# Inverse gate products of a gated recurrence: one reciprocal per token, or products from the far end of a segment

## The chip, the cores and the metric

The kernel runs on one core of a Trainium2 chip. The metric is the device time of one execution in microseconds, as the median of several runs. A profile of one execution is read beside it.

## The reference

The kernel computes one layer of a diffusion trunk: 2048 latent tokens of width 1024 and 256 context tokens, an HGRN2 gated linear recurrence in both directions, and a gated ConvFFN with final normalization. The edit lies in the recurrence. For each of 8 heads and each direction, with gates f in (0, 1) per token and feature and k = 1 - f:

```
f = lb[d] + (1.0 - lb[d]) * sigmoid(zf)          # logf = log(f), k = 1.0 - f
b = cumsum(logf)                                  # inside a chunk
scores = (q * exp(b - b_ref)) @ (k * exp(b_ref - b))^T      # masked, lower triangle
o_intra = scores @ v
kv = (k * exp(b_last - b))^T @ v                  # what the chunk adds to the state
s = exp(b_last) * s + kv                          # state, carried over the chunks
o = o_intra + (q * exp(b)) @ s_start
```

exp(b) is a running product of gates. The kernel computes these products directly, without logarithms, in segments of 32 tokens, and puts the segments together with products of segment totals.

## The kernel before, in words

The whole kernel is one body in a tile framework. The source order gives priorities; the framework's scheduler lays out the order of the instructions on each engine from modelled times and readiness, adds the semaphores, and places the tiles. So an instruction can stand earlier or later on its engine than in the source, and each engine then runs its own list in order.

The body has three stages. First a short preparation (modulation vectors, normalizing and transposing the first token tiles). Then the scan stage, `mixer_scan`: two groups of three units, each unit 384 tokens (three tiles of 128), and for each group all 8 heads, so 48 units. In the first group the first unit holds two context tiles and one latent tile (`s0` = 2, `g0` = 8), so 8 of the units have 4 latent segments and the other 40 have 12. Last come the readout with the output projection, and the ConvFFN. Weights and token tiles are split into a high and a low part (`split`: a ScalarE copy, L80, and a VectorE subtraction, L81), and each product is three matmuls (`mm3`, L350 to L352).

A `unit` does this. TensorE projects the tokens to gates for both directions (L380), ScalarE takes the sigmoid into `F` (L382), VectorE scales and shifts it (L384). `F` has for each direction 12 segments of 33 columns: column 0 is constant 1, columns 1 to 32 are the gates, in reversed token order for direction 1. TensorE projects `q`; ScalarE and VectorE make it silu (L419, L420). A VectorE scan along `F` (L428) with `d1`, which is 1 at column 0 of each segment and 0 elsewhere, gives `S`: the running products, starting anew at 1 in every segment. `ke` (L433, L434) is the difference of neighbouring columns of `S`, which is the key times the running product. `R` (L439) is the reciprocal of `S` at columns 0 to 31, taken in pieces of four segments; `qe` (L442, L443) is `q` times `R`; `qp` is `qe` times the segment total, column 32 of `S`. GpSimd (POOL) makes the products of segment totals `TB` and `TX` (L451 to L462) and `sd`. From them come `kd`, `qi`, `qm` and `km`, all by `scaled` (L467), a VectorE product with a broadcast scalar per segment. Then TensorE makes the values `v` and the gate (`values`), and `part_a` and `part_b` of each token tile, queued as a list of steps that the next unit runs between its own products (`fill`): transposes of `kd` (L517, `tr`), the scores `sc` from `ke` and `qe` (L525, L526), from `kx` and `qp` (L531), from `km` and `qm` (L532), their merging by masks into `at` (L536 to L541), the state's addition `kv` (L549), the output `o` (L564, L565) and the state `Sf` (L568). The results go to a stash in DRAM by DMA (L576 to L578).

New token tiles are prepared among these steps by `make_h`: a DMA loads `xt`, ScalarE sums the squares, `rms_scale` works out the factor with a small VectorE operation (L76) and a power on POOL (L77), ScalarE scales the tile (L103), TensorE transposes it into `tp` (L112), ScalarE and VectorE evacuate it as `hm` (L116, L119), and `split` makes `hh` and `hl`.

Of the kernel before, what the change touches and what calls it, by code (L numbers as in the profile page):

```python
# [9 lines left out]
F32 = mybir.dt.float32  # L10
# [4 lines left out]
OP = mybir.AluOpType  # L15
# [29 lines left out]
NS = 12  # L45
SEG = 33


def body(ctx, tc, a, out):
    nc = tc.nc  # L50
    pe, act, dve, pool, sp = nc.tensor, nc.scalar, nc.vector, nc.gpsimd, nc.sync
# [38 lines left out]
    def pool_(stack, name, bufs=1, **kw):  # L90
        return stack.enter_context(tc.tile_pool(name=name, bufs=bufs, reuse_waits="tile", **kw))
# [187 lines left out]
    def mixer_scan():  # L279
        gp = pool_(c1, "gp", side="right")  # L280
# [27 lines left out]
        d1 = fix.tile([128, NS, SEG], BF16, name="d1")  # L308
# [45 lines left out]
        def unit(h, w, u, tiles, todo):  # L354
# [4 lines left out]
            g0 = 4 * s0  # L359
            lat = slice(g0, NS)  # L360
# [4 lines left out]
            F = Fs[slot]  # L365
# [60 lines left out]
            S = gp.tile([128, 2, NS, SEG], F32, name="S", tag="S")  # L426
            for d in range(2):
# [5 lines left out]
            dve.tensor_tensor(ke[:, 0], S[:, 0, :, 0:32], S[:, 0, :, 1:SEG], OP.subtract)  # L433
            dve.tensor_tensor(ke[:, 1, :, 31::-1], S[:, 1, :, 0:32], S[:, 1, :, 1:SEG],  # L434
                              OP.subtract)
            R = gp.tile([128, 2, NS, 32], F32, name="R", tag="R")
            for d in range(2):
                for i in range(g0, NS, 4):
                    dve.reciprocal(R[:, d, i:i + 4], S[:, d, i:i + 4, 0:32])  # L439
            qe = gp.tile([128, 2, NS, 32], F32, name="qe", tag="qe", bufs=2)  # L440
            qv = q.rearrange("p (c t) -> p c t", t=32)
            dve.tensor_tensor(qe[:, 0, lat], qv, R[:, 0, lat], OP.mult)  # L442
            dve.tensor_tensor(qe[:, 1, lat], qv, R[:, 1, lat, 31::-1], OP.mult)  # L443

# [17 lines left out]
            def scaled(dst, src, w):  # L464

                w = w[..., None].to_broadcast(list(w.shape) + [32])
                dve.tensor_tensor(dst, src, w, OP.mult)  # L467
# [7 lines left out]
            scaled(kd, ke, TBf[:, 0:4:3])  # L475


            qp = gp.tile([128, 2, NS, 32], F32, name="qp", tag="qp", bufs=2)
            scaled(qp[:, :, lat], qe[:, :, lat], S[:, :, lat, 32])
            qi = gp.tile([128, 2, NS, 32], F32, name="qi", tag="qi", bufs=2)  # L480
            scaled(qi[:, :, lat], qp[:, :, lat], TBf[:, 1:3, lat])

# [145 lines left out]
        for g, units in enumerate(GROUPS):  # L628
            for h in range(NH):
                if g == h == 0:  # L630
                    w = head0
                else:
                    w = load_feat(h)
                    load_vg(h, w)
                for u, tiles in enumerate(units):
                    todo = list(unit(h, w, u, tiles, todo))
                    if h > 0 and steps < 16 * (g + 1):
                        next(rest, None)
                        steps += 1
                    if g == h == u == 0:  # L640
                        todo = with_h(todo, [f for i, t in enumerate(units[2]) for f in
                                             make_h(2, i, t, None if i else staged[6])])
                    if g == 0 and h == NH - 1:
                        todo = with_h(todo, [f for i, t in enumerate(GROUPS[1][u])
                                             for f in make_h(u, i, t)])
                    if g == 1 and h == NH - 1:
                        if u == 0:
                            todo.append(gate1)
                        for j, k in enumerate(range(3 * u, min(3 * u + 3, KT))):
                            todo.insert(len(todo) if u < 2 else j,  # L650
                                        lambda k=k: out_weight(k))
# [661 lines left out]
    S = V = None  # L1313
    for s in range(N):
        ph, c = divmod(s, NC)
        if s == 4:
# [4 lines left out]
            S = wk.tile([128, NC, HT, 128], F32, name="S")  # L1321
# [76 lines left out]
```

## Time and profile before

| | |
|---|---|
| time, median of 3 runs | 2870.17 us (2866.94 to 2872.55) |
| the profiled execution's own time | 2867.78 us |
| its span, first to last instruction | 2866.1 us |
| mean granted TensorE clock | 0.994 |
| busy: PE, PEld, DVE, ACT, POOL | 98%, 87%, 78%, 41%, 18% of the span |
| L439, reciprocals `R` on DVE | 256, 222.9 us |
| L428, forward scans `S` on DVE | 96, 93.9 us |

PE is TensorE's matmuls, PEld its weight loads, DVE is VectorE, ACT ScalarE, POOL GpSimd and SP the engine that issues most DMAs. Durations of the page are from the one profiled execution; the own time of that execution is 1.7 us more than its span. A row of a group gives line, engine, operation, output and inputs, shapes and count, then busy microseconds, the mean nanoseconds of one, and the idle time of the engine just before them with what ended it. A row of a timeline begins with start and length in microseconds.

### The profile page before, as it was taken

The numbers are of one execution on the slowest core, as the hardware profiler recorded it, in microseconds if no ns is written. First come the engines' busy times: TensorE is split into PE (matmuls) and PEld (weight loads), VectorE is DVE, ScalarE is ACT, GpSimd is POOL, SyncE is SP. The second block draws the span as 40 slices with busy tenths as digits, with TensorE's granted clock in tenths as the row PEclk, the third lists the DMA queues.
The fourth block names the chain that finished last, engine by engine and source line by source line (L and its number), as shares of the span: only waits on it lengthen the run. The fifth ranks groups of instructions, "written<-read, shape, count | busy, mean of one in ns | idle before, by whom it ended". The sixth has DMA issues, their size and how long they took to land.

```text
span 2866.1 us, 43816 instructions
## 1 busy us (share of the span) xinstructions
PE 2810.4 (98%) x16016; PEld 2507.1 (87%) x16016; DVE 2224.6 (78%) x3787; ACT 1169.4 (41%) x2500; POOL 528.5 (18%) x1028
## 2 busy tenths in 40 slices
PE   8999999999999999998999799999999999999999
PEld 4999999999999999997888688888888888887887
DVE  5777777778777777687898598887888887677887
ACT  4433333346333323333455444444444444433343
POOL 2101111111101001011111353443434432000001
PEclk9999999999999999999999899999999999999999
DMA  5222222223222222235777622224522224897663
GB/s 229 67 77 81 78 78 85 71 77 105 84 90 66 80 78 77 68 97 173 264 296 279 260 88 89 75 88 170 212 84 71 81 89 128 287 302 250 199 200 121
DMA packets 202912, 386.57 MB, mean 135 GB/s; under 512 B 26692, under 2 KB 117828, under 8 KB 197448
## 3 DMA queue, kind: packets, MB, share of 16 engines
q1 hardware_dynamic: 199960, 375.51, 38.9%
q10 hardware_dynamic: 2736, 8.26, 0.8%
q8 instruction: 126, 2.06, 0.3%
q14 instruction: 90, 0.74, 0.1%
HBM read 281.70 MB, written 101.99 MB: 134 GB/s over the span
## 4 chain that ended last, share of the span: by engine, by line
PE 85%; DMA 6%; DVE 5%; ACT 2%; issue 1%; POOL 1%; SPq 0%; DVEq 0%; ACTq 0%; POOLq 0%
PE z L350 10%; PE z L352 10%; PE z L351 10%; PE zd L710 3%; PE zd L707 3%; PE zd L709 3%; PE zc L710 3%; PE zc L707 3%; PE zc L709 3%; PE za L710 3%; PE za L707 3%; PE za L709 3%; PE y L1232 2%; PE y L1230 2%; PE y L1231 2%; PE kv L549 2%
## 5 line engine op out<-in xcount | busy, mean ns | idle before, releaser
L350 PE MATMUL z<-vh,hh 128*128 128x256 f32 (+1 forms) x1024 | 300.0, 293 | 0.0
L352 PE MATMUL z<-vh,hl 128*128 128x256 f32 (+1 forms) x1024 | 293.7, 287 | 0.0
L351 PE MATMUL z<-vl,hh 128*128 128x256 f32 (+1 forms) x1024 | 293.3, 286 | 0.0
L350 PE MATMUL z<-hh,wh 128*128 128x384 f32 x768 | 263.4, 343 | 3.4 <-ACT hh L80 3.4
L351 PE MATMUL z<-hl,wh 128*128 128x384 f32 x768 | 259.0, 337 | 1.1 <-DVE rs L76 0.6
L352 PE MATMUL z<-hh,wl 128*128 128x384 f32 x768 | 259.1, 337 | 0.0
L1232 PE MATMUL y<-wd,ml 128*128 128x512 f32 x600 | 234.0, 390 | 1.5 <-DVE ml L81 1.4
L1230 PE MATMUL y<-wd,mh 128*128 128x512 f32 x600 | 233.6, 389 | 0.7 <-DVE P L1284 0.7
L1231 PE MATMUL y<-wd,mh 128*128 128x512 f32 x600 | 233.5, 389 | 0.0
L439 DVE RECIPROCAL R<-S 128x128 f32<-128x128 f32 x256 | 222.9, 914 | 0.0
L350 PEld LDWEIGHTS z<-vh,hh 128*128 128x128 f32 x1024 | 196.3, 192 | 0.0
L351 PEld LDWEIGHTS z<-vl,hh 128*128 128x128 f32 x1024 | 196.1, 192 | 0.0
L352 PEld LDWEIGHTS z<-vh,hl 128*128 128x128 f32 x1024 | 195.8, 191 | 0.0
L81 DVE TENSOR_TENSOR w<-s,w 128x512 fp32r<-128x512 f32 x132 | 145.9, 1112 | 60.5 <-ACT w L80 60.5
L459 POOL COPY TX<-S 128x3 f32<-128x3 f32 x48 | 15.3, 318 | 812.4 <-DVE S L428 812.4
L81 DVE TENSOR_TENSOR w<-raw,w 128x512 fp32r<-128x512 f32 x176 | 123.6, 705 | 40.0 <-ACT w L80 39.6
L80 ACT ACTIVATE w<-raw 128x512 fp32r<-128x512 f32 x176 | 108.8, 626 | 111.3 <-DMA raw<-in_w_up_dram 43.3
L350 PEld LDWEIGHTS z<-hh,wh 128*128 128x128 f32 x768 | 145.2, 189 | 8.0 <-ACT hh L80 4.6
L994 DVE SCALAR_TENSOR_TENSOR r<-uv,conv,r 128x1023 f32<-128x1023 f32 (+1 forms) x88 | 149.3, 1715 | 0.4
L351 PEld LDWEIGHTS z<-hl,wh 128*128 128x128 f32 x768 | 145.3, 189 | 2.0 <-DVE hl L81 2.0
L399 ACT ACTIVATE v<-z 128x128 f32<-128x128 f32 x128 | 35.3, 276 | 273.5 <-PE z L352 273.5
L352 PEld LDWEIGHTS z<-hh,wl 128*128 128x128 f32 x768 | 144.9, 189 | 0.0
(324 smaller groups left out, 8024.6 us busy)
## 6 DMA issues: line engine op xcount, KB each, us to landing
raw<-in_w_up_dram SPq DMA_DIRECT2D x90, 512.0 KB, 4.0
raw<-in_w_in_dram SPq DMA_DIRECT2D x80, 512.0 KB, 3.7
lr<-m SPq DMA_DIRECT2D x49, 512.0 KB, 5.6
m<-r SPq DMA_DIRECT2D x66, 256.0 KB, 4.4
raw<-in_w_ada_dram SPq DMA_DIRECT2D x32, 512.0 KB, 4.4
stash<-st SPq DMA_DIRECT2D x125, 128.0 KB, 1.8
kq<-stash SPq DMA_DIRECT2D x15, 1024.0 KB, 7.5
og<-stash SPq DMA_DIRECT2D x15, 1024.0 KB, 6.5
```

The lines of the kernel that those rows point to most:

```text
L81: dve.tensor_tensor(l, src, h.bitcast(F32), OP.subtract)
L350: pe.matmul(o, sh[:, k], mh[:, k], start=k == 0, stop=False)
L351: pe.matmul(o, sh[:, k], ml[:, k], start=False, stop=False)
L352: pe.matmul(o, sl[:, k], mh[:, k], start=False, stop=k == KT - 1)
L439: dve.reciprocal(R[:, d, i:i + 4], S[:, d, i:i + 4, 0:32])
L707: pe.matmul(o, w[:, 0, k], r[:, :, 0, k], start=start and k == 0, stop=False, skip_group_check=True)
L709: pe.matmul(o, w[:, 0, k], r[:, :, 1, k], start=False, stop=False, skip_group_check=True)
L710: pe.matmul(o, w[:, 1, k], r[:, :, 0, k], start=False, stop=k == 3, skip_group_check=True)
L994: dve.scalar_tensor_tensor(r, x, cw, r, OP.mult, OP.add)
L1230: pe.matmul(z, lh, rh, start=start, stop=False, skip_group_check=True)
L1231: pe.matmul(z, lh, rl, start=False, stop=False, skip_group_check=True)
L1232: pe.matmul(z, ll, rh, start=False, stop=stop, skip_group_check=True)
```

## The change

After `S` has been made, `F` is scanned a second time, from the last column to the first and in place, with `d1` read backward too. Since `d1` is 0 except at column 0, where it is 1, and the product there cannot exceed 1, column t of each segment then holds the product of the gates from t to 32, and column 0 is 1 again. `qp`, formerly `q` times the inverse of the product so far times the segment total, is now `q` times that product from the other end. `qe` is `qp` times `rt`, one reciprocal of the segment total for each of the latent segments. The tile `R` is gone; `rt` is a small tile of 24 columns.

```
-            R = gp.tile([128, 2, NS, 32], F32, name="R", tag="R")
             for d in range(2):
-                for i in range(g0, NS, 4):
-                    dve.reciprocal(R[:, d, i:i + 4], S[:, d, i:i + 4, 0:32])
-            qe = gp.tile([128, 2, NS, 32], F32, name="qe", tag="qe", bufs=2)
+                Fr = F[:, d, lat].rearrange("p c t -> p (c t)")[:, ::-1]
+                dr_ = d1[:, lat].rearrange("p c t -> p (c t)")[:, ::-1]
+                dve.tensor_tensor_scan(Fr, Fr, dr_, 1.0, OP.mult, OP.max)
+            rt = gp.tile([128, 2, NS], F32, name="rt", tag="rt", bufs=2)
+            dve.reciprocal(rt[:, :, lat], S[:, :, lat, 32])
+
+            qp = gp.tile([128, 2, NS, 32], F32, name="qp", tag="qp", bufs=2)
             qv = q.rearrange("p (c t) -> p c t", t=32)
-            dve.tensor_tensor(qe[:, 0, lat], qv, R[:, 0, lat], OP.mult)
-            dve.tensor_tensor(qe[:, 1, lat], qv, R[:, 1, lat, 31::-1], OP.mult)
+            dve.tensor_tensor(qp[:, 0, lat], qv, F[:, 0, lat, 1:SEG], OP.mult)
+            dve.tensor_tensor(qp[:, 1, lat], qv, F[:, 1, lat, 32:0:-1], OP.mult)
...
-            qp = gp.tile([128, 2, NS, 32], F32, name="qp", tag="qp", bufs=2)
-            scaled(qp[:, :, lat], qe[:, :, lat], S[:, :, lat, 32])
+            qe = gp.tile([128, 2, NS, 32], F32, name="qe", tag="qe", bufs=2)
+            scaled(qe[:, :, lat], qp[:, :, lat], rt[:, :, lat])
```

## The prediction

> **What bounds the kernel now.** I read the busy times of the page first, then the busy time by stretches of the span, then the list of what TensorE waited for.
>
> ```profile
> PE 2810.4 (98%) x16016; PEld 2507.1 (87%) x16016; DVE 2224.6 (78%) x3787; ACT 1169.4 (41%) x2500; POOL 528.5 (18%) x1028
> ```
>
> TensorE is the busiest engine and VectorE the second. The shares are averages over three stages, and the edit lies in the first alone: the scan stage, whose units run from 54 us to 1330 us. Its stretches, with length, then busy time of PE, weight loads, DVE, ACT and POOL, and at the end the granted clock, the DMA share and rate:
>
> ```profile
> 54.00:100.00 46.00, 41.35 (x271) 38.13 (x270) 36.36 (x77) 23.44 (x58) 7.01 (x26) 0.96 0.07 22
> 100.00:595.00 495.00, 494.66 (x3504) 488.14 (x3503) 365.12 (x771) 171.14 (x522) 52.39 (x241) 1.00 0.26 81
> 595.00:695.00 100.00, 95.85 (x689) 92.37 (x687) 79.43 (x175) 60.93 (x147) 13.45 (x44) 1.00 0.29 92
> 695.00:1290.00 595.00, 594.41 (x4303) 587.88 (x4302) 455.33 (x936) 200.03 (x614) 56.73 (x264) 1.00 0.25 79
> 1290.00:1330.00 40.00, 38.64 (x290) 37.69 (x289) 33.41 (x70) 16.52 (x49) 4.20 (x14) 1.00 0.35 119
> ```
>
> In the two long stretches TensorE stands still for 0.34 and 0.59 us, and its weight loads alone fill 99% of them, while VectorE has a quarter of its time free. The idle time sits in three places: the first units (46.00 - 41.35 = 4.65 us), the switch to the second group of token tiles (4.15), the end of the stage (1.36). Together with the two long stretches it is 11.1 us. What ended each wait of TensorE in the stage (total us, times, longest):
>
> ```profile
> PE tp L112 <- ACT xt L103: 5.7, 9, 1.1
> PE tp L112 <- DVE hm L119: 1.8, 3, 0.9
> PE tp L112 <- ACT hm L116: 1.2, 1, 1.2
> PE tr L517 <- ACT kt L519: 0.8, 1, 0.8
> PE kv L549 <- DVE Sf L568: 0.6, 1, 0.6
> PE z L503 <- ACT vt L500: 0.5, 1, 0.5
> PE z L350 <- ACT hh L80: 0.4, 2, 0.2
> ```
>
> They sum to 11.0 us, the same total. None names an operation that the edit touches: most are the transposes `tp` of new token tiles, waiting for a tile to be normalized or for the evacuation before it.
>
> **The change, part by part.** It takes out the 256 reciprocals of L439, adds 96 backward scans and 48 short reciprocals, and exchanges the places of `qe` and `qp`. The groups that price it (count, then busy us, mean ns of one, idle before):
>
> ```profile
> L439 DVE RECIPROCAL R<-S 128x128 f32<-128x128 f32 x256 | 222.9, 914 | 0.0
> ...
> L428 DVE TENSOR_TENSOR_SCAN S<-F,d 128x396 f32<-128x396 f32 x96 | 93.9, 978 | 4.6 <-DVE F L384 0.9
> ...
> L467 DVE TENSOR_TENSOR qp<-qe,S 128x768 f32<-128x768 f32 x40 | 37.9, 949 | 0.4
> ...
> L434 DVE TENSOR_TENSOR ke<-S 128x384 f32<-128x384 f32 x48 | 27.0, 563 | 0.2
> L433 DVE TENSOR_TENSOR ke<-S 128x384 f32<-128x384 f32 x48 | 26.8, 559 | 0.4
> ...
> L467 DVE TENSOR_TENSOR km<-ke,TX 128x192 f32<-128x192 f32 x80 | 26.1, 327 | 0.0
> ...
> L442 DVE TENSOR_TENSOR qe<-q,R 128x384 f32<-128x384 f32 x40 | 21.8, 544 | 0.0
> ...
> L250 DVE RECIPROCAL mx<-mx 128x16 f32<-128x16 f32 x1 | 0.3, 252 | 0.0
> ```
>
> Removed: 222.9 us of VectorE, 6 x 914 = 5.48 us in each of the 40 full units and 2 x 914 = 1.83 us in each of the 8 units with two context tiles.
>
> Added, the scans: 80 have the 396 columns of L428, 80 x 978 = 78.2 us. That a scan runs from the far end and over its own input is shown nowhere; the floor I see is a forward scan, 978 ns, and the ceiling is twice that if it read badly. I take 978, because reversing costs a neighbour nothing (L434 is the operation of L433 with a reversed output, 563 ns beside 559). The 16 short ones have 132 columns: between a third of 978, 326 ns, and 978; I take 400, near the proportional end, 16 x 400 = 6.4 us. [...]
>
> Added, the short reciprocals: 16 columns took 252 ns and 128 took 914, a slope of 5.9 ns a column, so 24 columns are about 299 ns (x40 = 12.0 us) and 8 columns, extrapolated, 205 ns (x8 = 1.6 us).
>
> Moved: the two products with `q` now read F at segments of 33 columns instead of R at 32; L433 reads both operands so and takes 559 ns against 544, at most 0.015 x 80 = 1.2 us. `qe` becomes the broadcast product that `qp` was, 949 ns either way. No DMA, no matrix product and no ScalarE operation is added or moved in the source.
>
> VectorE thus saves 222.9 - 78.2 - 6.4 - 12.0 - 1.6 - 1.2 = 123.5 us, about 3.2 us in a full unit; with scans at twice the price it would still save some 39.
>
> What of this is on the path? A full unit from the middle of the stage, VectorE's rows and then TensorE's first products that use its results:
>
> ```profile
> 1114.94 2.56 DVE L439 RECIPROCAL R<-S 128x128 f32<-128x128 f32 x3
> ...
> 1117.86 0.96 DVE L467 TENSOR_TENSOR kd<-ke,TB 128x768 f32<-128x768 f32 x1
> ...
> 1123.32 0.62 DVE L467 TENSOR_TENSOR qm<-qp,TX 128x192 f32<-128x192 f32 x2
> ```
>
> ```profile
> 1133.08 0.38 PE L517 MATMUL tr<-ident,kd 128*128 128x128 f32 x2
> ...
> 1133.96 0.39 PE L532 MATMUL sc<-qm,km 128*128 128x128 f32 x2
> ```
>
> `kd` is ready 14.3 us before its transposes start, and the last product `qm` 10.0 us before `sc` reads it. Between lie the 72 matmuls of the unit's values. So the removed 3.2 us end in slack, and a chain longer by up to 10 us would too: I cost the steady units at 0 on both sides.
>
> Three places remain. In the first unit:
>
> ```profile
> 62.69 0.94 DVE L439 RECIPROCAL R<-S 128x128 f32<-128x128 f32 x1
> ...
> 64.89 1.22 DVE L81 TENSOR_TENSOR hl<-hm,hh 128x1024 fp32r<-128x1024 f32 x1
> ```
>
> ```profile
> 63.58 1.08 ACT L80 ACTIVATE hh<-hm 128x1024 fp32r<-128x1024 f32 x1
> ```
>
> `hl` starts 0.2 us after ScalarE's `hh` is done at 64.66, so a shorter reciprocal ahead of it brings 0.2 us there. The transposes wait 1.8 us in all on `hm` of VectorE. I take 0.5, bounds 0 and 1.8.
>
> At the group switch the chain that ended last passes through reciprocals (start, us, what):
>
> ```profile
> 604.99 1.71 DVE R L439 x2
> ...
> 611.78 0.81 DVE R L439
> ...
> 616.12 0.55 POOL rs L77
> ...
> 649.90 1.00 POOL rs L77
> ```
>
> 2.5 us of L439 lie there ahead of the first new tile; behind it the chain is normalizing, x-tile loads and transposes. What is late next is ScalarE's `xt`, whose waits are 5.7 us over nine tiles. I take 1.0, bounds -1 and 4.15, the whole idle time of this stretch.
>
> At the end:
>
> ```profile
> 1309.43 2.57 DVE L439 RECIPROCAL R<-S 128x128 f32<-128x128 f32 x3
> ...
> 1312.91 0.56 DVE L420 TENSOR_TENSOR q<-z,q 128x384 f32<-128x384 f32 x1
> ```
>
> `q` waits for TensorE's product, and it is needed after the change as before; only the two `km` products (2 x 327 ns) can slide ahead of it into the freed time. I take 0.5, bounds 0 and 1.36.
>
> The sum: 0.5 + 1.0 + 0.5 = 2.0 us. The profiled execution took 2867.78 us (span 2866.1 and 1.7 around it) and would take 2865.8. The median of the runs shown is 2870.17, 2.4 above it, so I forecast 2868.2.
>
> VectorE's work also holds POOL off, and that is where the edit could cost:
>
> ```profile
> 115.31 0.18 POOL L462 COPY TX<-S 128x3 f32<-128x3 f32 x1
> ...
> 119.32 1.58 POOL L451 COPY TB<-S 128x6 f32<-128x6 f32 x1 [3.83 <-DVE S L428]
> ```
>
> ```profile
> 115.23 2.57 DVE L439 RECIPROCAL R<-S 128x128 f32<-128x128 f32 x3
> ...
> 119.18 1.20 DVE L81 TENSOR_TENSOR wl<-raw,wh 128x1024 fp32r<-128x1024 f32 x1
> 120.30 0.55 DVE L434 TENSOR_TENSOR ke<-S 128x384 f32<-128x384 f32 x1
> ```
>
> A tiny copy takes 0.18 us beside a reciprocal (one input) and 1.58 us beside two operations with two inputs: it ends with them. The edit puts two-input scans where one-input reciprocals stood, so POOL loses 2.57 us of open time per direction and meets 0.98 us of closed time instead. [...] For `TB` this is harmless: it has the 14.3 us of slack of `kd`, and what queues behind `kd` on VectorE is the same unit's work, with 10 us.
>
> **The rivals.** Faster by over 0.2% (a measurement of this kernel cannot tell less than about 0.2%, 5.7 us, from no change): VectorE's free time, and the new order that the scheduler lays out from modelled times, let the new token tiles come early at both ends, and two thirds of the 11.1 us go: 7.4 us, 2862.8 us; all of it would be 2859.1. For it: reciprocals stand on the chain at the switch. Against it: most of these waits name ScalarE.
>
> Slower: POOL's power `rs` (L77) lies on the chain of every new token tile, between the sum of squares and ScalarE's `xt`; it took 0.55 us at 616 and 1.00 at 649. If a scan (0.98 us) covers it at the nine places where TensorE already waits for `xt`, each wait grows by that: 9 x 0.98 = 8.8 us, 2868.2 + 8.8 = 2877.0. It decides from 7.7 / 9 = 0.86 us on each, the forecast gain included. [...] Against it: only some of the tiles meet a scan, which is one operation among many with two inputs.
>
> That VectorE saves nothing, because a backward scan is several times dearer, changes the sum little: the slack covers 10 us in a unit, and 2870 us would stay.
>
> **How the numbers follow.** Forecast with its bounds (within 0.2%, 2864.4 to 2875.9): 0.52, since the long stretches leave VectorE nothing to give. Faster rival 0.28: it needs half of the idle time. Slower rival 0.20. The range goes from 2861.0, beyond the two-thirds case, to 2878.0, beyond the slower rival.
>
> **What would show it.** Right: the reciprocal group of 223 us gone, a scan group of 96 at 0.9 to 1.1 us beside L428, VectorE some 120 us less busy, TensorE's busy time and the stage's end within 3 us of now. Wrong: a stage end before 1325 or after 1335 us; a list of TensorE's waits in which `sc`, `tr` or `o` name VectorE; `rs` of POOL above its mean of now with longer `tp` waits.

## The result and the profile after

The kernel after took 2878.18 us (median of seven runs, 2877.13 to 2879.91). The kernel before took 2869.56 us (median of seven runs, 2866.94 to 2872.55), so the ratio is 1.003, 95% interval 1.0019 to 1.0042. It is slower by 8.6 us, just outside the range and 1.2 us from where the slower rival put it (2877.0).

VectorE did become freer, as forecast. First the busy times of the page after, then its new groups:

```profile
PE 2812.5 (98%) x16016; PEld 2508.9 (87%) x16016; DVE 2109.9 (73%) x3675; ACT 1170.6 (41%) x2500; POOL 587.6 (20%) x1028
```

```profile
L441 DVE TENSOR_TENSOR_SCAN F<-F,d 128x396 f32<-128x396 f32 x80 | 78.0, 975 | 0.0
L443 DVE RECIPROCAL rt<-S 128x24 f32<-128x24 f32 x40 | 11.0, 275 | 0.0
...
L472 DVE TENSOR_TENSOR kd<-ke,TB 128x768 f32<-128x768 f32 x48 | 45.9, 956 | 31.0 <-PE tr L522 22.2 <-POOL TB L462 8.9
```

A backward scan in place costs 975 ns, as much as a forward one (979). VectorE is 114.7 us less busy, and TensorE's busy time grew by 2.1 us only. POOL's grew by 59.1 us though no POOL instruction was touched. The last row shows where part of the freed time went: VectorE stands idle for 31.0 us ahead of `kd`, where it stood 4.0 us before. Of this 8.9 us are waits for POOL's `TB`.

Three stretches of the scan stage after (columns as in the prediction):

```profile
100.00:595.00 495.00, 493.86 (x3494) 486.92 (x3493) 323.37 (x731) 171.38 (x521) 78.96 (x241) 1.00 0.26 81
595.00:695.00 100.00, 92.26 (x657) 88.87 (x656) 70.98 (x167) 57.74 (x140) 16.40 (x43) 0.98 0.28 88
695.00:1290.00 595.00, 593.75 (x4295) 587.11 (x4294) 392.35 (x868) 202.84 (x619) 78.32 (x260) 1.00 0.26 80
```

In the long stretches VectorE's busy time fell by 42 and 63 us and TensorE's stayed within 0.8. At the group switch (second row) TensorE is idle for 7.74 us instead of 4.15, and the granted clock is 0.98 instead of 1.00.

How far the kernel after has fallen behind is read from the start of a unit's sigmoid on ScalarE (units 22, 27 and 47; the rows begin with start and length), first before, then after:

```profile
601.52 0.49 ACT L382 ACTIVATE F<-z 128x384 f32<-128x384 f32 x1 [3.86 <-PE z L352]
...
750.38 0.49 ACT L382 ACTIVATE F<-z 128x384 f32<-128x384 f32 x1 [1.68 <-PE z L352]
...
1298.75 0.49 ACT L382 ACTIVATE F<-z 128x384 f32<-128x384 f32 x1 [1.95 <-PE z L352]
```

```profile
603.60 0.49 ACT L382 ACTIVATE F<-z 128x384 f32<-128x384 f32 x1 [3.86 <-PE z L352]
...
757.42 0.49 ACT L382 ACTIVATE F<-z 128x384 f32<-128x384 f32 x1 [1.83 <-PE z L352]
...
1306.38 0.49 ACT L382 ACTIVATE F<-z 128x384 f32<-128x384 f32 x1 [1.95 <-PE z L352]
```

2.08 us are lost by unit 22, 7.04 by unit 27, 7.63 by unit 47. So the start costs 2.1 and the switch 5.0. Then the lateness stays at 7.0 up to unit 46 and grows by 0.6 at unit 47; the last `o` of the stage starts 8.3 us late (1338.06 against 1329.80). The profiled spans differ by 10.4; the other 2.1 lie in stages whose source is the same, and I do not assign them. The 10.4 is more than the 8.6 of the medians because the profiled execution of the kernel before took 1.8 us less than its median.

**The switch.** The new tile that TensorE waits for, on ScalarE, VectorE, POOL and TensorE, before:

```profile
669.54 1.06 ACT L100 ACTIVATE junk<-xt 128x1024 f32<-128x1024 f32 x1
...
671.31 0.13 DVE L76 TENSOR_SCALAR rs<-ss 128x1 f32<-128x1 f32 x1
...
671.98 0.55 POOL L77 TENSOR_TENSOR rs<-rs,mhalf 128x1 f32<-128x1 f32 x1
672.49 1.00 POOL L452 TENSOR_TENSOR TB<-TB,S 128x6 f32<-128x6 f32 x1
...
673.76 0.66 PE L112 MATMUL tp<-ident,xt 128*128 128x128 f32 x4 [1.11 <-ACT xt L103]
```

And after:

```profile
670.92 1.19 DVE L81 TENSOR_TENSOR hl<-hm,hh 128x1024 fp32r<-128x1024 f32 x1
...
672.15 1.06 ACT L100 ACTIVATE junk<-xt 128x1024 f32<-128x1024 f32 x1 [0.59 <-DVE hl L81]
...
673.73 0.59 POOL L456 COPY TB<-S 128x6 f32<-128x6 f32 x1 [4.52 <-DVE S L428]
...
674.18 0.15 DVE L76 TENSOR_SCALAR rs<-ss 128x1 f32<-128x1 f32 x1
...
675.09 0.97 DVE L441 TENSOR_TENSOR_SCAN F<-F,d 128x396 f32<-128x396 f32 x1
...
675.14 0.93 POOL L462 TENSOR_TENSOR TB<-TB,S 128x6 f32<-128x6 f32 x1
676.03 0.29 POOL L459 TENSOR_TENSOR sd<-TB,S 128x6 f32<-128x6 f32 x1
676.38 0.34 POOL L463 COPY decb<-sd 128x3 f32<-128x3 f32 x1
676.68 0.54 POOL L77 TENSOR_TENSOR rs<-rs,mhalf 128x1 f32<-128x1 f32 x1
...
678.45 1.11 PE L112 MATMUL tp<-ident,xt 128*128 128x128 f32 x4 [3.33 <-ACT xt L103]
```

The new schedule places `rs` of POOL behind the whole chain of `TB`, `sd` and `decb`, where the old one had it in the middle. The new scan at 675.09 stretches one product of that chain to 0.93 us (its neighbours take 0.21), and `rs` starts 2.35 us after L76 has ended. From the first copy of the chain at 673.73 to `rs` are 2.95 us. In e9 below, where no scan runs beside it, the same ten operations take 1.69 us (674.11 to 675.80). By this estimate some 1.3 us of the 2.35 come from VectorE's two-input operations that hold POOL (the first copy takes 0.59 us for 0.19 in e9, the product beside the scan 0.93 for 0.21), and the rest from the place behind the chain. The lateness grows from 2.61 us at L100 and 2.87 at L76 to 4.70 at `rs`, and TensorE waits 3.33 us. Then its granted clock drops to 0.50. The stretch behind that wait, and the steps of 384-column products in it and behind it:

```profile
678.20:681.60 3.40, 3.15 (x11) 3.15 (x12) 1.36 (x4) 0.20 (x1) 0.00 (x0) 0.50 0.00 0
```

```profile
680.33 0.52 PE L351 MATMUL z<-hl,vh 128*128 128x384 f32 x1
680.64 0.52 PE L352 MATMUL z<-hh,vl 128*128 128x384 f32 x1
...
681.97 0.34 PE L351 MATMUL z<-hl,vh 128*128 128x384 f32 x1
682.14 0.34 PE L352 MATMUL z<-hh,vl 128*128 128x384 f32 x1
...
682.32 0.60 PE L112 MATMUL tp<-ident,xt 128*128 128x128 f32 x4
```

At a granted clock of 0.50 a product follows the last after 0.31 us, else after 0.17. The next `tp` at 682.32 stood at 676.17 before, 6.15 us earlier: the half clock has added about 1.45 us to the 4.69. The stretch of 3.40 us at 0.50 begins behind the wait of 3.33 us; shorter waits are taken up in the last section.

**The start.** VectorE, POOL and TensorE in unit 3, after:

```profile
121.18 0.97 DVE L441 TENSOR_TENSOR_SCAN F<-F,d 128x396 f32<-128x396 f32 x1
...
123.08 0.96 DVE L472 TENSOR_TENSOR kd<-ke,TB 128x768 f32<-128x768 f32 x1 [0.73 <-POOL TB L462]
...
124.42 0.34 DVE L573 SCALAR_TENSOR_TENSOR Sf<-Sf,sd,kv 128x128 f32<-128x128 f32 x1
```

```profile
121.25 0.89 POOL L460 COPY TB<-S 128x6 f32<-128x6 f32 x1
...
124.81 0.71 PE L554 MATMUL kv<-v,kt 128*128 128x128 f32 x4 [0.50 <-DVE Sf L573]
```

The second copy of `TB`, 0.19 us long in the kernel before (at 120.84), takes 0.89 us beside the scan, `kd` waits 0.73 us for the chain, and the update of the state `Sf` is queued behind `kd` on VectorE. TensorE waits 0.50 us for it. In the kernel before `Sf` stood ahead of the reciprocals (at 121.49) and of `kd` (at 124.84):

```profile
121.23 0.34 DVE L568 SCALAR_TENSOR_TENSOR Sf<-Sf,sd,kv 128x128 f32<-128x128 f32 x1
```

### The profile page after: what moved, and what is told of

The parts are those of the page before. It is cut to its first block, busy times and chain, and to the rows that moved or that the text cites. A ratio compares the mean times of both kernels' runs of the same rounds, so it can differ in the third digit from the quotient of the medians.

```text
span 2876.5 us, 43715 instructions
## 1 busy us (share of the span) xinstructions
PE 2812.5 (98%) x16016; PEld 2508.9 (87%) x16016; DVE 2109.9 (73%) x3675; ACT 1170.6 (41%) x2500; POOL 587.6 (20%) x1028
## 4 chain that ended last, share of the span: by engine, by line
PE 85%; DMA 6%; DVE 5%; ACT 2%; issue 1%; POOL 1%; SPq 0%; DVEq 0%; POOLq 0%; ACTq 0%
PE z L351 10%; PE z L352 10%; PE z L350 10%; PE zd L712 3%; PE zc L712 3%; PE zc L715 3%; PE zd L715 3%; PE zc L714 3%; PE zd L714 3%; PE za L712 3%; PE za L715 3%; PE za L714 3%; PE y L1237 2%; PE y L1235 2%; PE y L1236 2%; PE kv L554 2%
## 5 line engine op out<-in xcount | busy, mean ns | idle before, releaser
L404 DVE TENSOR_TENSOR st<-z,st 128x128 f32<-128x128 f32 x127 | 36.4, 287 | 157.8 <-ACT st L403 157.8
```

## The experiments

The theory: two-input scans lengthen POOL's chain, and since the schedule now has `rs` behind that chain, new token tiles come late. Rivals: the order alone; the hold of the scans on POOL alone, wherever `rs` stands; or a new limit that has nothing to do with POOL. In the table "start" is the lateness of unit 22's sigmoid against the kernel before, and "switch" what is added up to unit 27's, from each profile as above.

| kernel | median us | ratio to before, 95% | start us | switch us |
|---|---|---|---|---|
| after | 2878.18 | 1.003 (1.0019 to 1.0042) | 2.1 | 5.0 |
| e1, one input | 2869.78 | 0.9999 (0.999 to 1.0008) | 0.1 | 0.4 |
| e2, order pinned | 2873.75 | 1.0013 (1.0003 to 1.0022) | 1.1 | 1.3 |
| e3, old form at switch | 2873.73 | 1.0014 (1.0004 to 1.0023) | 1.0 | 0.4 |
| e4, chain on VectorE | 2871.24 | 1.0003 (0.9994 to 1.0013) | -0.1 | 1.2 |
| e5, before, two inputs | 2871.69 | 1.0007 (0.9998 to 1.0016) | 4.4 | -0.5 |
| e6, after, second x tile | 2876.87 | 1.0027 (1.0017 to 1.0036) | 2.5 | 4.4 |
| e7, before, second x tile | 2868.59 | 0.9997 (0.9988 to 1.0006) | 1.6 | -0.3 |
| e8, e4 and second x tile | 2869.31 | 1.0 (0.9991 to 1.001) | 0.9 | 0.8 |
| e9, after, own square buffer | 2872.81 | 1.0014 (1.0005 to 1.0023) | 1.4 | 1.3 |
| e10, before, own square buffer | 2868.65 | 1.0001 (0.9992 to 1.001) | 0.2 | 0.8 |
| e11, e4 and own square buffer | 2871.74 | 1.0006 (0.9998 to 1.0015) | 1.5 | 4.0 |
| e12, e4 and both buffers | 2862.49 | 0.9976 (0.9967 to 0.9985) | -0.3 | -4.1 |
| e13, before and both buffers | 2861.98 | 0.9973 (0.9964 to 0.9983) | 0.6 | -5.0 |
| e14, after and both buffers | 2866.47 | 0.9992 (0.9983 to 1.0001) | 0.9 | -3.8 |
| e15, before, chain on VectorE, both | 2864.56 | 0.9987 (0.9978 to 0.9996) | -0.3 | -3.5 |

Both columns rest on one profiled execution of each kernel. Those of e2, e3 and e4 took 2.6 to 2.9 us less than their medians, so the columns need not add up to the difference of the medians. The start holds something that is not the edit: between 44 and 60 us, mostly ahead of the first scan, the granted clock was 0.79 after and 0.89 before, and from 54 to 100 us it was 0.96 in both and 1.00 in e3 and e4. Differences of about 1 us in this column are therefore not read as effects.

**One input instead of two (e1).** Each backward scan becomes a reciprocal in place, of about the same length:

```
-                dve.tensor_tensor_scan(Fr, Fr, dr_, 1.0, OP.mult, OP.max)
+                dve.reciprocal(F[:, d, g0:g0 + 4], F[:, d, g0:g0 + 4])
...
-            dve.reciprocal(rt[:, :, lat], S[:, :, lat, 32])
+            dve.reciprocal(rt[:, :, lat], F[:, :, lat, 0])
```

> The changed kernel with each backward scan replaced by an in-place reciprocal of 132 gate columns (one input, some 0.9 us), and the short reciprocal taken of the constant column 0 of F: the products from the other end and the inverse totals are left out. The order of POOL's operations stays that of the changed kernel, with the factor rs of a new tile behind the whole TB chain at the group switch. Theory port (two-input scans hold POOL off): POOL's TB operations fall back to the durations of before, decb from 0.52 to about 0.19 us, the rs of the switch comes at least 1 us earlier, the step at the switch shrinks from 5.0 us to 3 or less, time about 2875. Theory order (rs stands behind the chain whatever its length): the step stays between 4 and 5 us, time about 2877.

POOL's groups between 54 and 1335 us, in the kernel before, after, and in e1:

```profile
L451 POOL COPY TB<-S 128x6 f32<-128x6 f32 x48 | 19.3, 403 | 240.4 <-DVE S L428 233.6 <-DVE rs L76 6.7
...
L458 POOL COPY decb<-sd 128x3 f32<-128x3 f32 x40 | 7.5, 186 | 2.5
```

```profile
L456 POOL COPY TB<-S 128x6 f32<-128x6 f32 x48 | 30.3, 632 | 232.4 <-DVE S L428 232.4
L463 POOL COPY decb<-sd 128x3 f32<-128x3 f32 x40 | 20.9, 523 | 2.5
```

```profile
L455 POOL COPY TB<-S 128x6 f32<-128x6 f32 x48 | 22.9, 478 | 238.4 <-DVE S L428 238.4
...
L462 POOL COPY decb<-sd 128x3 f32<-128x3 f32 x40 | 9.8, 244 | 2.5
```

The whole loss is gone, which is more than either theory expected, and the shorter work of VectorE by itself costs nothing that can be measured. POOL's copies are shorter again. At the switch `decb` takes 0.19 us (at 673.46) beside the reciprocal that starts at 673.25 and takes 0.96; beside the scan above, of 0.97 us, the second copy of `TB` took 0.89. The mean of `decb` is 244 ns here and 523 in the kernel after.

At the switch, however, e1 does not separate the hold on POOL from the order. The row of L76 and the ends of POOL's chain there:

```profile
672.99 0.14 DVE L76 TENSOR_SCALAR rs<-ss 128x1 f32<-128x1 f32 x1
```

```profile
670.67 1.11 POOL L455 COPY TB<-S 128x6 f32<-128x6 f32 x1 [6.11 <-DVE S L428]
...
673.60 0.55 POOL L77 TENSOR_TENSOR rs<-rs,mhalf 128x1 f32<-128x1 f32 x1
```

`rs` still stands behind the chain, and the chain is as long as in the kernel after (2.93 us against 2.95). But it begins 2.46 us ahead of the end of L76, where in the kernel after it begins 0.60 ahead, so `rs` starts 0.47 us after L76 and not 2.35. The reason is VectorE's order: in e1 the forward scan that the chain waits for stands ahead of `hl` (669.63 and 670.52), in the kernel after behind it (672.70 and 670.92). At the start too e1 has another order, with `Sf` ahead of `kd`. So e1 clears the freed time of VectorE, but what the place behind the chain would cost without the scans stays open.

**The order undone (e2), and the old form at the switch (e3).** e2 keeps the change and places the tail of the chain behind `rs` in the units of the switch; e3 gives the three units of the last head of the first group their reciprocals back.

```
+            with tc.issue_after(own[0].ins) if own else ExitStack():
+                pool.tensor_tensor(pre[:, :, :, 2], pre[:, :, :, 1], tot[:, :, :, 1], OP.mult)
...
+            old = h == NH - 1 and tiles[0] < 7
+            if old:
+                R = gp.tile([128, 2, NS, 32], F32, name="R", tag="R")
```

> The changed kernel with one edge more in the two switch units that load new tiles: the tail of POOL's TB chain is issued behind the rs of the unit's first new tile, the order that the kernel before had. Theory order: the wait of 3.3 us for xt falls to about 1.3, the half-clock stretch behind it goes, the step at the switch falls from 5.0 us to 2 or less, time about 2875. Theory port: rs still meets the scans, the step falls by less than 1 us, time about 2877. If the cost at the switch has another cause (place of the tiles in memory, the x load), nothing changes.

> The changed kernel with the form of before (reciprocals R) in the three units of the last head of group 0 alone; the other 45 units keep the change. If the cost sits at the switch: step there 0 to 1 us, the start keeps its 2.1 us, time about 2873. If the change costs in every unit or through the stage's memory layout: about 2878.

Both regain 4.4 us against the kernel after. In e3 that is three units of 48, so the switch is where half of the loss is made. In e2 VectorE's operations at the switch stand in the order of the kernel after, the scans that hold POOL are still there (a copy takes 0.88 us beside the one at 674.21), and `rs` starts 0.19 us after L76: 3.7 of the switch's 5.0 us are gone. So the place of `rs` behind the chain is needed for this loss at the switch. It is not the whole loss: with the order undone e2 is still 4.1 us slower than before. That the scans' hold cost its share of the switch rests on the estimate of 1.3 us above and not on a run of its own.

**POOL's chain on VectorE (e4), and two inputs in the kernel before (e5).**

```
-            pool.tensor_copy(pre[:, :, :, 1], tot[:, :, :, 0])
+            dve.tensor_copy(pre[:, :, :, 1], tot[:, :, :, 0])
...
-                for i in range(g0, NS, 4):
-                    dve.reciprocal(R[:, d, i:i + 4], S[:, d, i:i + 4, 0:32])
+                for i in range(5 if not s0 else 2):
+                    dve.tensor_tensor(R[:, d], S[:, d, :, 0:32], S[:, d, :, 1:SEG], OP.mult)
```

> The changed kernel with the eleven products and copies of segment totals (TB, TX, sd, decb) moved from POOL to VectorE, so that POOL has only the rs powers in the stage. Both theories: rs has no chain ahead of it, at most one VectorE operation holds it off, so the step at the switch falls to 1 us or less and the start may lose part of its 2.1 us; time 2871 to 2874. VectorE gets some 1.6 us a unit back, inside its 10 us of slack. If TensorE's waits at the switch stay at 7 us, POOL was not the cause and VectorE's own order was.

> The kernel before with each set of three reciprocals (2.57 us, one input) replaced by five products of 384 columns with two inputs (about 0.55 us each, two products where the unit has context tiles); the inverse products are left out, R holds a product instead. VectorE's busy time stays near that of before. Theory port: POOL now has some 5.5 us of closed time per unit more, its TB operations get longer than in the changed kernel or equal, the rs of the switch and sd come late, and the kernel is slower than before by 4 us or more, 2874 to 2885. Rival (what costs is VectorE's new order or the missing interleaving, not the port): within 2 us of before.

With all twelve small operations on VectorE the kernel is level with before (the interval includes 1), so nearly all of the loss goes through POOL's chain. Here `Sf` stands ahead of `kd` again at the start. e5 came out 2.9 us above its runs of before, between the 4 or more of the theory and the 2 of its rival; the interval includes 1, so it decides nothing. Its first copy of `TB` takes 906 ns on average, for 632 in the kernel after and 403 in the one before:

```profile
L451 POOL COPY TB<-S 128x6 f32<-128x6 f32 x48 | 43.5, 906 | 250.6 <-DVE S L428 248.8 <-DVE rs L76 1.8
```

Yet nothing is lost at its switch, where `rs` is not behind the chain. Its late start (4.4) was not taken apart.

**What makes the square late: buffers (e6 to e11).** The tile `xt` has one buffer, so its load waits for the transposes of the last tile; and the discarded squares `junk` share one buffer with `hm`, so L100 waits for `hl`. I first took the load for the limit.

```
-                got[0] = x_tile(xp, t)
+                got[0] = x_tile(xp, t, bufs=2)
...
-                junk = xp.tile([128, D], F32, name="junk", tag="hm")
+                junk = xp.tile([128, D], F32, name="junk", tag="junk")
```

> The changed kernel with two buffers instead of one for the token tile xt (and the accumulator that shares its tag), so that a tile can be loaded and normalized while the one before is still transposed. Theory port plus chain: the rs of a tile has a tile's time of slack, so POOL's delay no longer reaches TensorE: the waits of tp for xt fall from 8.1 us to 3 or less, the step at the switch to 0 or below, time 2868 to 2873. If the x load was not the neck, 2877.

> The kernel before with two xt buffers. Its 5.7 us of waits for xt fall to 2 or less; time 2864 to 2868. Rival: scaling a tile on ScalarE sets the pace at the switch, then 2869.

> The changed kernel with the segment totals' products on VectorE and two xt buffers: POOL has neither a queue nor a chain in the stage. Theory: the best of the changed forms, 2863 to 2868, equal to or below the kernel before with two buffers. Rival: 2869 or more, if ScalarE sets the pace at the switch.

The second tile alone did nothing in the kernel after: the longest wait for `xt` stayed 3.3 us, and the row of L100 above names `hl`, not the load. e7 and e8 came out near their rivals' 2869; that ScalarE sets the pace, the rivals' reason, was not shown. So the square's own buffer was next:

> The kernel after, with a buffer of its own (4 KB per partition) for the squares that ScalarE throws away (L100), which shared one buffer with `hm` and so waited for VectorE's `hl`. If the 5 us at the group switch are the late `rs` behind POOL's chain, the square can now start some 2 us sooner, `rs` gets ahead of or into the chain, the 3.3 us wait of `tp` for `xt` falls to 1 or 2, and the time to 2872 to 2875. If the scans' hold on POOL is the whole cause wherever `rs` stands, 2877 to 2879 stays.

> The kernel before with the same separate buffer. Its nine `tp` waits for `xt` are 5.7 us in all; if the wait for `hl` made half of them, 2866 to 2868; if the sums come early enough there already, no change within 0.1%.

> The kernel after with the products of segment totals on VectorE and the separate buffer. POOL then does hardly more than `rs`, and neither the chain nor `hl` holds it. If those two were what is left at the new tiles, 2864 to 2867, ahead of both kernels; if TensorE's own work bounds all the rest, as before, 2868 to 2871.

In e9 `rs` gets ahead of the chain without any pin, the longest wait is 1.3 us, and 5.4 us of the loss are gone:

```profile
669.28 0.12 DVE L76 TENSOR_SCALAR rs<-ss 128x1 f32<-128x1 f32 x1
```

```profile
669.69 0.54 POOL L77 TENSOR_TENSOR rs<-rs,mhalf 128x1 f32<-128x1 f32 x1
...
674.11 0.19 POOL L456 COPY TB<-S 128x6 f32<-128x6 f32 x1 [3.88 <-DVE S L428]
...
675.61 0.19 POOL L463 COPY decb<-sd 128x3 f32<-128x3 f32 x1
```

e10 gained nothing. e11 missed both of its figures; one tile earlier it meets the other limit, the load, and again a stretch at a granted clock of 0.50 (shown in the last section):

```profile
659.32 1.06 ACT L100 ACTIVATE junk<-xt 128x1024 f32<-128x1024 f32 x1 [2.19 <-DMA xt<-in_x_dram]
```

```profile
662.58 1.11 PE L112 MATMUL tp<-ident,xt 128*128 128x128 f32 x4 [2.27 <-ACT xt L103]
```

**Both buffers (e12 to e15).** The two limits stand one behind the other, so I removed both: in e4's kernel, in before, in after, and in before with the chain on VectorE.

> The kernel after with the products of segment totals on VectorE, a separate buffer for the squares and a second buffer for the x tile: all three things that held the new tile's scaling at the group switch (POOL's chain, `hl`, and the load of the tile) are taken away together. If these waits are what is left to gain at the new tiles, the waits of `tp` for `xt`, 5.4 to 6.2 us so far, fall to 1 or 2 us and the time to 2864 to 2867. If another limit stands right behind them (ScalarE's own queue, TensorE's order), they stay above 4 us and the time is 2868 to 2871.

> The kernel before with the two buffers alone (a second x tile, a separate buffer for the squares). If the gain of the version with all three changes comes from the buffers, 2862 to 2865. If the reciprocals on VectorE still hold the new tile's scaling, or POOL's chain does, 2866 to 2869.

> The kernel after with the two buffers alone; POOL keeps the products of segment totals beside the two-input scans. If the late power on POOL needs the late square that the shared buffers make, the gain is whole: 2862 to 2865. If POOL's chain costs also where the square comes early, 2866 to 2872.

> The kernel before with the two buffers and the products of segment totals on VectorE: the version with all three, without the change itself. If the change's freed VectorE time is worth nothing even there, 2862 to 2864, as with the change; if the freed 2.7 us a unit are what gives VectorE the room for those products, 2866 to 2870.

The switch in e12, e13 and e14:

```profile
595.00:695.00 100.00, 98.35 (x709) 96.22 (x708) 77.52 (x207) 62.62 (x152) 4.45 (x7) 1.00 0.30 92
```

```profile
595.00:695.00 100.00, 98.98 (x716) 96.95 (x715) 82.96 (x182) 62.48 (x151) 13.58 (x45) 1.00 0.28 90
```

```profile
595.00:695.00 100.00, 97.86 (x709) 95.75 (x709) 74.75 (x171) 62.29 (x151) 16.66 (x43) 1.00 0.30 93
```

TensorE's 4.15 us of idle time at the switch shrink to 1.65, 1.02 and 2.14, and no `tp` waits for `xt` any more. e13, the kernel before with 8 KB more of buffers per partition, is 7.7 us faster than before and needs nothing of the change. With the same buffers the change costs 4.5 us (e14 against e13), even where the square is early: the waits of `kv` for `Sf` are 1.8 us there and 0.6 in e13. Taking the chain off POOL brings the changed kernel to e13's time (e12). So this cost too goes through POOL's chain; whether by the scans' hold or by VectorE's order with `kd` ahead of `Sf` was not separated. In the kernel before the same move brought nothing (e15 is 2.6 us above e13). e12 lies 2.1 us below e15, but their intervals overlap, so VectorE's freed time shows no sure gain in any pair.

## Why the prediction was wrong

*VectorE saves 123.5 us.* Right in its terms: scans 84.8 us for 84.6 forecast, short reciprocals 12.4 for 13.6. These give 125.7 less, and the busy time fell by 114.7, since VectorE's other operations took 11.0 more in all.

*Steady units at 0.* Right: the lateness stays at 7.0 us from unit 27 to unit 46, although the copies shown are on average 0.2 to 0.3 us longer.

*The start, a gain of 0.5.* Wrong sign: a loss of 2.1. 0.5 of it is TensorE's wait for `Sf` in unit 3, which e1 and e4 do not have; there `Sf` stands ahead of `kd`. The sentence that failed is that what queues behind `kd` on VectorE is the same unit's work, with 10 us of slack: without the reciprocals, which had covered POOL's chain, `kd` stands ahead of `Sf`, for which TensorE's next `kv` waits. The rest of the 2.1 is not settled: the clock ahead of the first scan differs between the runs, and e7, without the change, shows 1.6.

*The switch, a gain of 1.0 with bounds -1 and 4.15.* This is the failed term: it lost 5.0, beyond the bound of 1 us of loss. It named ScalarE's `xt` as next in line and stopped there. `xt` waits for POOL's `rs`, and whether `rs` stands ahead of or behind a 3 us chain of POOL is the scheduler's choice, which this edit turned over. The slower rival did go on to `rs`, and the text had shown a copy held for 1.58 us, but neither entered the bound of this term.

*The end, a gain of 0.5.* Wrong sign: the lateness grows by 1.2 us between unit 46 and the last `o`. TensorE's `kv` waits for `Sf` three times there, about 0.6 us each, and once in the kernel before. It is the wait of the start again. The prediction's own signs of being wrong came with it: the stage ends after 1335 us, and POOL's `rs` rose from a mean of 614 ns in the stage to 700, with longer `tp` waits.

*The slower rival.* Right in engine and instruction, wrong in the mechanism's course: not nine waits with 0.98 us more each, but one wait of 3.33 us and the half clock behind it. That its 2877.0 came so close is luck, since start, switch and end share the loss and only the switch is its own. Its chance, 0.20, leaned on "only some of the tiles meet a scan"; one tile behind the whole chain was enough. That it could get its place from a new order was not said.

*The faster rival.* The two thirds of the idle time do exist (e13 gains 7.7 us), but VectorE does not hold them: buffers do.

## What to carry to other kernels

Before VectorE's work is made cheaper, look at which engine its operations hold off: here a small copy of POOL ran in 0.19 us beside a one-input reciprocal of 0.96 us and another took 0.89 beside a two-input scan of 0.97, so a shorter form can make an engine late that nobody edited. An edit that frees an engine off the path can still reorder the others' queues, so follow a critical wait through every link to its last one and ask what stands ahead of that instruction on its engine. Where a wait has two limits in series (here a buffer shared with `hm` and a single tile for the load), removing one may show nothing; try both before the gain is written off. And when an experiment exchanges one operation for another, compare the order on every engine before its result is put down to the operation: e1 moved a scan ahead of `hl`.

## What the runs showed of the hardware

A scan read backward and written in place takes 975 ns for 396 columns, a forward one 979. The sixteen of 132 columns take 425 ns, which by an estimate from these two lengths makes about 2.1 ns a column and some 150 ns besides. Reciprocals of 24 columns take 275 ns, below the 299 on the line from 16 columns (252) to 128 (914). A wait of 2.27 us (e11) was followed by a stretch at a granted clock of 0.50:

```profile
662.60:666.00 3.40, 3.40 (x12) 3.40 (x13) 2.56 (x6) 2.15 (x4) 0.00 (x0) 0.50 0.00 0
```

The length of one wait does not by itself decide this. Waits of up to 1.4 us (e4, e9) brought no such stretch at the switch, and e12 to e14 had none there: the granted clock was 1.00 over it in all five. But in the kernel after, where no wait between 54 and 74 us is longer than 1.30 us, the clock was 0.51 from 74 to 76 us, and in the kernel before, where none between 54 and 72 us is longer than 1.16, it was 0.50 from 72 to 74. What decides it is not settled here.
